# The up-projection of a feed-forward layer as seven block products per column pair, with the gated rows kept in memory

## Chip, core and metric

The kernel runs on one core of a Trainium2 chip. The metric is device microseconds of one execution. Engines are named as the profile names them: PE is the tensor engine (PEld its weight loads), DVE the vector engine, ACT the scalar engine, POOL the GpSimd engine, SP the engine that issues most transfers.

## What is computed

One layer of a decoder trunk for 1024 prompt tokens and 8 decode rows: a normalised input x, three token mixers, a layer norm, then a gated feed-forward with a causal convolution of width 3 over its up-projected rows, and a second layer norm. The change is in the feed-forward; the reference has it as

```
def conv_ffn(x, buf, w_up, conv_w, conv_b, w_down):
    hup = x @ w_up
    ext = jnp.concatenate([buf.astype(hup.dtype), hup], axis=1)
    c = ext[:, 0:L] * conv_w[0] + ext[:, 1:L + 1] * conv_w[1] + ext[:, 2:L + 2] * conv_w[2] + conv_b
    a, b = jnp.split(c, 2, axis=-1)
    return (jax.nn.gelu(a) * b) @ w_down, ext[:, -(CONV_WIDTH - 1):]
...
    x = layer_norm(ALPHA * x + f, ln2_g, ln2_b)
```

x has 1024 features, hup 2 x 2816 columns, so there are 22 feature tiles of 128 for a and 22 for b. All data is float32.

## The kernel before

Tokens stand side by side in 1032 columns (1024 and the 8 decode rows), features on the 128 partitions. Every float32 factor of a large product is split into two parts of 12 bits, hi and lo: ACT copies the source to the short type (hi), DVE or POOL subtracts it (lo). A product is then three matmuls, hi by hi, hi by lo, lo by hi. xhi and xlo hold x's parts in eight feature tiles.

The program is written as a list of units. A unit is 128 output columns: for each of three token chunks (384, 384, 264) it adds eight k-tiles times three matmuls into one PSUM bank, and then a function empties the bank. run_units goes through them; between matmuls it loads weights (a 512 KB piece, SP), splits them (whi on ACT, line 180; wlo, line 181, mostly on DVE, on POOL for a few stages) and advances side work, given as generators in lanes. The order on each engine is the order in which the program writes it; each engine works through its queue in order. Three banks, tag "d", go round under the units; units marked wide use others as well.

The stages: memory keys and values, input projection and mLSTM, attention, gates, pooling, w_o with the first layer norm, feed-forward, second layer norm. The gates are written to memory by POOL's transfers (line 1117) and come back later. to_features writes the normalised rows into xhi and xlo.

In the feed-forward an up unit (up_unit) empties its bank twice on ACT, as hup (line 1490) and as cv with the convolution's last tap and bias (line 1491). convolved then adds the other taps on DVE (line 1503, two instructions of about 1023 columns, and two of 8 for the decode rows), takes gelu on ACT for the a tile (line 1506), multiplies on POOL for the b tile (line 1509), copies hup's last columns on POOL (line 1500) and splits the gated tile into GH (lines 1523, 1524), which stay in SBUF. Up units and down units are mixed: after four feature tiles' gates, eight down units of four k-tiles (36 matmuls each) add to z2 (lines 1539 to 1544). The pool named rows, 21 tiles of 128x1032, holds the gates, z2 and cv.

## Time and profile before

| What | us |
|---|---|
| median of 3 runs (2214.75 to 2216.33) | 2214.9 |
| span of the profiled execution | 2210.3 |
| PE busy in it | 2169.0 |
| DVE busy | 1207.6 |
| ACT busy | 826.1 |
| POOL busy | 364.5 |

The span runs from the first to the last instruction of the profiled execution, whose mean granted clock is 0.994. Rows of the chain of waits and of the timeline give the start in us, the duration in us, and what ran; xN means N instructions in a row. Groups give count, busy us and mean ns of one, then the idle time ahead of them and what ended it. Rows by window give, after the length, the sum busy and then PE, PEld, DVE, ACT and POOL, with the count of instructions in brackets, the granted clock, the share of transfer engines and GB/s. The feed-forward runs from about 1405 to 2118 us.

### The profile page before, as it was taken

How to read it: one execution, taken by the hardware profiler on the slowest of the kernel's cores; microseconds unless marked ns; L12 is line 12 of the kernel's file. 1: busy time of each engine (PE TensorE's matmuls, PEld its weight loads, DVE VectorE, ACT ScalarE, POOL GpSimd, SP SyncE). 2: the span in 40 equal slices, each digit the busy share in tenths (PEclk: the TensorE clock that was granted, in tenths of full speed). 3: DMA queues.
4: the chain of work that ended last, by engine and by line, in shares of the span. 5: the costliest groups of instructions: out<-in, count | busy, mean ns of one | idle time of the engine just before them, and what ended most of it. 6: DMA issues, size and time to landing. Idle time of an engine off the chain costs nothing.

```text
span 2210.3 us, 36109 instructions
## 1 busy us (share of the span) xinstructions
PE 2169.0 (98%) x14337; PEld 2140.7 (97%) x14337; DVE 1207.6 (55%) x2776; ACT 826.1 (37%) x1635; POOL 364.5 (16%) x523
## 2 busy tenths in 40 slices
PE   8999999999999999999999999999999999999996
PEld 7899999999999999999999999999999999999996
DVE  6834738383767765635335556644544343443457
ACT  4524343434457543442213333444142341423421
POOL 6301010101110000211004734101010010101104
PEclk9999999999999999999999999999999999999998
DMA  9131232223367664649653223311111111111112
GB/s 264 55 106 53 58 72 53 63 61 70 90 187 260 193 193 159 217 173 339 189 165 103 87 77 86 87 49 49 42 45 49 49 49 48 39 52 45 49 49 77
DMA packets 267795, 229.50 MB, mean 104 GB/s; under 512 B 15669, under 2 KB 245863, under 8 KB 267611
## 3 DMA queue, kind: packets, MB, share of 16 engines
q1 hardware_dynamic: 261291, 208.12, 31.4%
q0 software_dynamic: 6336, 19.09, 2.3%
q8 instruction: 112, 1.84, 0.3%
q14 instruction: 56, 0.46, 0.1%
HBM read 177.13 MB, written 50.64 MB: 103 GB/s over the span
## 4 chain that ended last, share of the span: by engine, by line
PE 88%; DVE 4%; issue 3%; DMA 1%; SPq 1%; ACT 1%; POOL 1%; ACTq 0%; DVEq 0%; POOLq 0%
PE pd L250 79%; PE ps L668 1%; PE ps L669 1%; PE ps L670 1%; DMA Cs<-in_state_C_dram 1%; SPq L171 1%; DVE xlo L387 1%; PE ps L692 1%; PE ps L1086 1%; PE ps L878 1%; PE ps L382 0%; DVE st L358 0%; DVE xhi L386 0%; DVE wlo L181 0%; PE ps L688 0%
## 5 line engine op out<-in xcount | busy, mean ns | idle before, releaser
L250 PE MATMUL pd<-xhi,whi 128*128 128x384 f32 (+1 forms) x2784 | 897.3, 322 | 0.6 <-ACT gf L541 0.6
L250 PE MATMUL pd<-xlo,whi 128*128 128x384 f32 (+1 forms) x2784 | 895.0, 321 | 0.0
L250 PE MATMUL pd<-xhi,wlo 128*128 128x384 f32 (+1 forms) x2784 | 891.2, 320 | 0.0
L250 PEld LDWEIGHTS pd<-xhi,whi 128*128 128x128 f32 x2784 | 524.5, 188 | 1.9 <-ACT gf L541 0.8
L250 PEld LDWEIGHTS pd<-xlo,whi 128*128 128x128 f32 x2784 | 524.9, 189 | 0.1
L250 PEld LDWEIGHTS pd<-xhi,wlo 128*128 128x128 f32 x2784 | 524.3, 188 | 0.0
L181 DVE TENSOR_TENSOR wlo<-raw,whi 128x512 fp32r<-128x512 f32 (+1 forms) x326 | 227.0, 730 | 437.2 <-ACT whi L180 430.6
L180 ACT ACTIVATE whi<-raw 128x512 fp32r<-128x512 f32 (+1 forms) x382 | 219.4, 620 | 271.6 <-PE pd L250 201.4
L1490 ACT ACTIVATE hup<-pd 128x384 f32<-128x384 f32 (+1 forms) x132 | 60.4, 458 | 277.9 <-PE pd L250 277.7
L1503 DVE SCALAR_TENSOR_TENSOR cv<-hup,colB,cv 128x1023 f32<-128x1023 f32 x88 | 112.7, 1281 | 1.6
L1544 DVE TENSOR_TENSOR z<-pd,z 128x384 f32<-128x384 f32 (+3 forms) x120 | 59.5, 511 | 82.6 <-PE pd L250 82.6
L1500 POOL COPY tl<-hup 128x10 f32<-128x10 f32 x44 | 8.4, 192 | 519.6 <-ACT hup L1490 519.6
L366 POOL TENSOR_TENSOR rs<-rs,half 128x1 f32<-128x1 f32 (+2 forms) x60 | 38.0, 633 | 340.2 <-DVE rs L365 330.1
L1491 ACT ACTIVATE cv<-pd,colB 128x384 f32<-128x384 f32 (+1 forms) x132 | 83.6, 633 | 0.0
L181 POOL TENSOR_TENSOR wlo<-raw,whi 128x512 fp32r<-128x512 f32 x56 | 76.3, 1386 | 41.4 <-ACT whi L180 41.4
L1117 POOL DMA_DIRECT2D gD<-ch x60 | 32.8, 547 | 293.5 <-ACT ch L1116 274.4
L1509 POOL TENSOR_TENSOR cv<-cv,cv 128x1032 f32<-128x1032 f32 x22 | 53.1, 2414 | 112.6 <-DVE cv L1503 97.0
L250 PE MATMUL pd<-mh,whi 128*128 128x392 f32 (+2 forms) x192 | 62.7, 326 | 0.6 <-ACT mh L1338 0.6
L250 PE MATMUL pd<-ml,whi 128*128 128x392 f32 (+2 forms) x192 | 61.8, 322 | 0.1
L250 PE MATMUL pd<-mh,wlo 128*128 128x392 f32 (+2 forms) x192 | 61.5, 321 | 0.0
L1116 ACT ACTIVATE ch<-pd,colA 128x384 f32<-128x384 f32 (+1 forms) x60 | 32.7, 545 | 67.1 <-PE pd L250 56.2
L662 ACT ACTIVATE hh<-ps,colA 128x128 fp32r<-128x128 f32 x64 | 23.1, 360 | 79.7 <-DVE hh L663 75.0
(731 smaller groups left out, 4040.9 us busy)
## 6 DMA issues: line engine op xcount, KB each, us to landing
raw<-in_w_in_dram SPq DMA_DIRECT2D x72, 512.0 KB
raw<-in_w_up_dram SPq DMA_DIRECT2D x44, 512.0 KB
raw<-in_w_down_dram SPq DMA_DIRECT2D x22, 512.0 KB
raw<-in_w_o_dram SPq DMA_DIRECT2D x18, 512.0 KB
mx<-mixD SPq DMA_DIRECT2D x16, 516.0 KB
raw<-in_w_mem_kv_dram SPq DMA_DIRECT2D x16, 512.0 KB
Cs<-in_state_C_dram SPq DMA_DIRECT2D x32, 256.0 KB
out_dram<-Cs SPq DMA_DIRECT2D x32, 256.0 KB
```

Source lines behind the costliest of these rows:

```text
L180: nc.scalar.activation(s.hi[:, ks], s.raw[:, ks], AF.Copy)
L181: (nc.gpsimd if s.pool else nc.vector).tensor_sub(s.lo[:, ks], s.raw[:, ks], raw_f(s.hi[:, ks]))
L250: nc.tensor.matmul(p[:u.m, :n], lhsT=a, rhs=b, start=j == 0, stop=j == len(seq) - 1)
L366: nc.gpsimd.tensor_tensor(out=rs[:n], in0=rs[:n], in1=half[:n], op=OP.pow)
L662: nc.scalar.activation(hi, src, AF.Copy, scale=scale)
L1116: nc.scalar.activation(t[:, :n], p[:, :n], AF.Identity, bias=bias)
L1117: nc.gpsimd.dma_start(GD[b][f][:, c0:c0 + n], t[:, :n])
L1490: nc.scalar.activation(rw[:, c0:c0 + n], p[:, :n], AF.Copy)
L1491: nc.scalar.activation(cc[:, c0:c0 + n], p[:, :n], AF.Identity, bias=colB[:, 132 + ft:133 + ft], scale=colB[:, 88 + ft:89 + ft])
L1503: nc.vector.scalar_tensor_tensor(a, b[0], b[1], a, op0=OP.mult, op1=OP.add)
L1509: nc.gpsimd.tensor_mul(cc, CA.pop(j), cc)
L1544: nc.vector.tensor_add(Z2[f][:, cs], p[:, :n], Z2[f][:, cs])
```

## The change

The first three feature tiles' up units (NSTD) stay as they were. Each of the other 19 pairs, column tile a and column tile b of one feature tile j, is now one product of a 2 x 2 block form: the rows of w_up are halved (512 features each), the columns are the a and the b tile, the tokens are halved (516 columns). Seven block products take the place of eight, in the form with shared sums: sums of weight blocks are built per pair on POOL (lines 1604, 1605, 1607, 1610 of the changed kernel), sums of token blocks once, on DVE and POOL (g_parts), each then split into two parts. Each product is done for two quarters s of 258 columns: seven products of four k-tiles and three matmuls (line 1733). Products 2 and 3 add onto the banks of products 1 and 5. ACT and DVE then empty the banks with the partial results as second factor (lines 1740 to 1755), into two hup tiles. The convolution starts from hup alone (line 1499 in ACT, 1505 on DVE, 1509 gelu, 1512 product on POOL).

The token sums overwrite half of xhi and xlo (last_part) and x1D, a copy in memory of the normalised rows, is written by ACT's transfers during the first layer norm. The gated tiles go to memory (gD, SP). When all pairs are done, the down products run in six groups: a group's gates come back into a stage tile, are split into xhi and xlo, and z2 starts from x1D. The weights' pool is one tag of eight tiles; rows is closed when the four last standard units begin, and five smaller pools take its place. Transfers of rowsA, of the gates and of y1 are issued by ACT and no longer by POOL, that of mixD by SP.

```diff
...
+NSTD = 3
+SEQ = (1, 6, 7, 5, 2, 4, 3)
+HB, HT = 258, 516
...
-    wp = ctx.enter_context(tc.tile_pool(name="weights", bufs=2))
-    hp = ctx.enter_context(tc.tile_pool(name="rows", bufs=NH))
+    wp = ctx.enter_context(tc.tile_pool(name="weights", bufs=8, side="right"))
+    sp = ctx.enter_context(tc.tile_pool(name="small", bufs=4))
+    early = ExitStack()
+    hp = early.enter_context(tc.tile_pool(name="rows", bufs=NH))
     pp = ctx.enter_context(tc.tile_pool(name="psum", bufs=1, space=bass.MemoryType.PSUM))
...
-            nc.gpsimd.dma_start(rowsA[dst:dst + n], as_rows(src))
+            nc.scalar.dma_start(rowsA[dst:dst + n], as_rows(src))
...
+            if spill:
+                nc.scalar.dma_start(spill[f][:, c0:c0 + n], tmp[:, :n])
...
-                nc.gpsimd.dma_start(GD[b][f][:, c0:c0 + n], t[:, :n])
+                nc.scalar.dma_start(GD[b][f][:, c0:c0 + n], t[:, :n])
...
+    def g_conv(j, isb, rw):
+
+        ft = j + NFF * isb
+        if j % 2 == 0 and not isb:
+            TL[j // 2] = sp.tile([128, 4, 10], F32, tag="tl", bufs=2, name=nm("tl"))
+        tl = TL[j // 2]
+        cc = R("cv")
+        w0, w1 = colB[:, ft:ft + 1], colB[:, 44 + ft:45 + ft]
+        nc.scalar.activation(cc, rw, AF.Identity, bias=colB[:, 132 + ft:133 + ft], scale=colB[:, 88 + ft:89 + ft])
+        nc.gpsimd.tensor_copy(tl[:, 2 * isb + j % 2, :], rw[:, T - 2:])
+        yield
+        steps = ((cc[:, 1:T], (rw[:, :T - 1], w1)), (cc[:, 2:T], (rw[:, :T - 2], w0)),
+                 (cc[:, T:], (stT[:, ft, 1, :], w1)), (cc[:, T:], (stT[:, ft, 0, :], w0)))
+        for i, (a, b) in enumerate(steps):
+            nc.vector.scalar_tensor_tensor(a, b[0], b[1], a, op0=OP.mult, op1=OP.add)
+            if i in (0, 3):
+                yield
+        if not isb:
+            nc.scalar.activation(cc, cc, AF.Gelu_apprx_tanh)
+            CA[j] = cc
+            return
+        nc.gpsimd.tensor_mul(cc, CA.pop(j), cc)
+        if j % 2:
...
+        yield
+        yield
+        nc.sync.dma_start(gD[j], cc)
...
+    def split_weights(o, key, src, pool):
+        slot = slots.pop(0)
+        t = (wp if slot == "w" else place["ex"]).tile([128, 1024], F32R, tag="w", name=nm("whl"))
+        n = src.shape[1]
+        hi, lo = t[:, :n], t[:, 512:512 + n]
+        nc.scalar.activation(hi, src, AF.Copy)
+        (nc.gpsimd if pool else nc.vector).tensor_sub(lo, src, raw_f(hi))
+        o.w[key] = [x.rearrange("p (k c) -> p k c", c=128) for x in (hi, lo)] + [slot]
+
...
+    def prepare():
+
+        if made["obj"] == made["load"] or not slots:
+            return False
+        o = wq[made["obj"]]
+        key = o.steps[made["step"]]
+        if o.pair:
+            add, sub = nc.gpsimd.tensor_add, nc.gpsimd.tensor_sub
+            if made["step"] == 0:
+                o.s = [wf_tile(), wf_tile()]
+            a11, a21, a22, a12 = o.f
+            s1, s2 = o.s
+            if made["step"] == 0:
+                add(s1, a21, a22)
+                sub(s2, s1, a11)
+            elif made["step"] == 1:
+                sub(a21, a11, a21)
+            split_weights(o, key, {1: a11, 6: s2, 7: a21, 5: s1, 2: a12, 4: a22, 3: a12}[key], key in (2, 4))
+            if key == 4:
+                sub(a12, a12, s2)
+        else:
+            split_weights(o, key, o.f[key], False)
+        made["step"] += 1
+        if made["step"] == len(o.steps):
+            made["step"] = 0
+            made["obj"] += 1
+            made["live"] -= o.nf
+            load_weights()
+        return True
+
+    def ready_weights(o, key):
+        while key not in o.w:
...
+    def x_part(m, k, s):
+        if m in (6, 7, 4):
+            a, b = TX[m]
+            return a[:, k, s * HB:(s + 1) * HB], b[:, k, s * HB:(s + 1) * HB]
+        kk, c0 = {1: (0, 0), 2: (4, 0), 3: (4, HT), 5: (0, HT)}[m]
+        c0 += s * HB
+        return xhi[:, kk + k, c0:c0 + HB], xlo[:, kk + k, c0:c0 + HB]
...
+    def open_ffn():
         wait_for("ln11")
...
+        flush()
+        ph.close()
+        early.close()
+        for name in ("t", "wf", "ex", "rc", "st"):
+            place[name] = ph.enter_context(tc.tile_pool(name=f"ffn_{name}", reuse_waits="tile",
+                                                        bufs={"t": 3, "wf": NWF, "ex": 2, "rc": 5, "st": 2}[name]))
+        cur[0] = place["rc"]
+        slots[:] = ["x", "x"]
+        made["live"] = 6
+        load_weights()
+        side.add(0, "parts", g_parts())
+        side.add(1, "first", g_first())
...
+    on(units[n0 + 4], "before", open_ffn)
...
+    def g_parts():
...
+        for k in range(4):
+            (h11, l11), (h12, l12), (h21, l21), (h22, l22) = (
+                [raw_f(x[:, k + 4 * a, b * HT:(b + 1) * HT]) for x in (xhi, xlo)] for a in range(2) for b in range(2))
+            t1, t2, t3 = wf_tile(HT), wf_tile(HT), wf_tile(HT)
+            T1.append(t1)
+
+            def split(m, src):
+                nc.scalar.activation(TX[m][0][:, k], src, AF.Copy)
+                V.tensor_sub(TX[m][1][:, k], src, raw_f(TX[m][0][:, k]))
+
+            P.tensor_sub(t3, h22, h12)
+            P.tensor_add(t3, t3, l22)
+            P.tensor_sub(t3, t3, l12)
+            V.tensor_sub(t1, h12, h11)
+            V.tensor_add(t1, t1, l12)
+            yield 2.0
+            V.tensor_sub(t1, t1, l11)
+            V.tensor_sub(t2, h22, t1)
+            V.tensor_add(t2, t2, l22)
+            yield 2.2
+            split(6, t2)
+            yield 1.5
+            split(7, t3)
+            P.tensor_sub(t2, h21, t2)
+            P.tensor_add(t2, t2, l21)
+            yield 2.0
+            split(4, t2)
...
+    def last_part():
+        for k in range(4):
+            h, l = xhi[:, k, HT:], xlo[:, k, HT:]
+            nc.scalar.activation(h, T1[k], AF.Copy)
+            nc.vector.tensor_sub(l, T1[k], raw_f(h))
+        made["live"] -= 4
...
+    class Pair:
+        def __init__(self, j):
+            self.j, self.hooks = j, {}
+            a, b = j * 128, FF + j * 128
+            q = lambda k, c: w_up[0, k * 512:(k + 1) * 512, c:c + 128].rearrange("(k p) c -> p k c", p=128)
+            self.w = Weights([q(0, a), q(0, b), q(1, b), q(1, a)], True)
+            wq.append(self.w)
...
+    def run_pair(u):
+        out = None
+        for s in range(2):
+            c1, c2 = slice(s * HB, (s + 1) * HB), slice(HT + s * HB, HT + (s + 1) * HB)
+            bank = {}
+            for i, m in enumerate(SEQ):
+                ready_weights(u.w, m)
+                onto = {2: 1, 3: 5}.get(m)
+                p = bank[m] = bank[onto] if onto else (
+                    pp.tile([128, 512], F32, tag="d", bufs=3, name=nm("pd")) if m in (1, 5) else PS("pd"))
+                wh, wl = u.w.w[m][:2]
+                for k in range(4):
+                    xh, xl = x_part(m, k, s)
+                    for n, (a, b) in enumerate(((wh, xh), (wh, xl), (wl, xh))):
+                        nc.tensor.matmul(p[:, :HB], lhsT=a[:, k], rhs=b, start=onto is None and k + n == 0,
+                                         stop=k == 3 and n == 2, skip_group_check=onto is not None)
+                if s:
+                    release(u.w, m)
+                p = p[:, :HB]
+                if m == 1:
+                    t1 = small("t1")
+                    nc.scalar.activation(t1, p, AF.Copy)
+                elif m == 6:
+                    u2 = small("u2")
+                    nc.vector.tensor_add(u2, p, t1)
+                elif m == 7:
+                    u3 = small("u3")
+                    nc.vector.tensor_add(u3, p, u2)
+                else:
+                    if out is None:
+                        out = [R("hup"), R("hup")]
+                    if m == 2:
+                        nc.scalar.activation(out[0][:, c1], p, AF.Copy)
+                    elif m == 3:
+                        nc.vector.tensor_add(out[0][:, c2], p, u2)
+                    else:
+                        nc.vector.tensor_add(out[1][:, c1 if m == 4 else c2], p, u3)
+                if (s, i) in u.hooks:
+                    u.hooks[s, i]()
+                post[:] = [g for g in post if next(g, g) is not g]
+                prepare()
+                side.advance(12 * HB / 2180.0)
+
+        def both():
+            yield from g_conv(u.j, 0, out[0])
+            yield from g_conv(u.j, 1, out[1])
+        post.append(both())
+
+
...
+    def stage_load(gi, parts):
+        j0, nk = GROUPS[gi]
+        if gi not in stage:
+            stage[gi] = place["t"].tile([128, 4, TT], F32, tag="t", name=nm("stage"))
+        for c0, c1 in parts:
+            for k in range(nk):
+                nc.sync.dma_start(stage[gi][:, k, c0:c1], gD[j0 + k][:, c0:c1])
+
+    def stage_split(gi, k, c0, c1):
+        kk = (gi % 2) * 4 + k
+        nc.scalar.activation(xhi[:, kk, c0:c1], stage[gi][:, k, c0:c1], AF.Copy)
+        nc.vector.tensor_sub(xlo[:, kk, c0:c1], stage[gi][:, k, c0:c1], raw_f(xhi[:, kk, c0:c1]))
...
+    def begin_down():
+        load_z2([0])
+        stage_load(0, ((384, TT),))
+        load_z2(range(1, 8))
+        side.add(0, "stages", g_stages())
+
+    pairs[-1].hooks = {(1, 1): lambda: stage_load(0, ((0, 384),)),
+                       (1, 5): lambda: stage_split(0, 0, 0, 384),
+                       (1, 6): lambda: [stage_split(0, k, 0, 384) for k in range(1, 4)]}
+    downs[0].before = begin_down
...
+            z = Z2[u.f][:, c0:c0 + n]
+            if u.gi == 0:
+                nc.vector.scalar_tensor_tensor(z, z, ALPHA, p[:, :n], op0=OP.mult, op1=OP.add)
+            else:
+                nc.vector.tensor_add(z, p[:, :n], z)
...
     run_units(2)
+    made["open"] = True
+    side.finish("parts")
+    slots.extend("www")
+    last_part()
+    load_weights()
+    for u in pairs:
+        run_pair(u)
+    for u in downs:
+        run_down(u)
...
```

POOL in the middle of the pairs, before (two up units; tl is the tail copy, cv the convolution):

```order
398 L1500 COPY tl_18417<-hup_18415 128x10
399 L1500 COPY tl_18417<-hup_18528 128x10
400 L1500 COPY tl_18417<-hup_18994 128x10
401 L1509 TENSOR_TENSOR cv_2932_18995<-cv_2875_18416,cv_2932_18995 128x1032
402 L1500 COPY tl_18417<-hup_19090 128x10
```

and of the change, one pair:

```order
399 L1500 COPY tl_19738<-hup_19525 128x10
400 L1500 COPY tl_19738<-hup_19526 128x10
401 L1512 TENSOR_TENSOR cv_19793<-cv_19739,cv_19793 128x1032
402 L1588 TENSOR_TENSOR whl_19875<-wf_19404,whl_19875 128x512
403 L1588 TENSOR_TENSOR whl_19893<-wf_19402,whl_19893 128x512
404 L1610 TENSOR_TENSOR wf_19404<-wf_19404,wf_19683 128x512
405 L1604 TENSOR_TENSOR wf_19935<-wf_19663,wf_19665 128x512
406 L1605 TENSOR_TENSOR wf_19936<-wf_19935,wf_19661 128x512
407 L1607 TENSOR_TENSOR wf_19663<-wf_19661,wf_19663 128x512
```

Behind the gate's product POOL now has six instructions on weights in each pair, where it had none (wf is a weight block or a sum of such, whl the two split parts).

DVE in a pair of the change, from the last sum of one pair into hup (L1753) through both convolutions of its two tiles; before, the convolutions (L1503) had only weight splits and the gate's split beside them:

```order
2236 L1753 TENSOR_TENSOR hup_19009<-pd_19128,u_3075_19103 128x258
2237 L1588 TENSOR_TENSOR whl_19204<-wf_18884,whl_19204 128x512
2238 L1743 TENSOR_TENSOR u_3097_19239<-pd_19226,t_3093_19220 128x258
2239 L1505 SCALAR_TENSOR_TENSOR cv_19223<-hup_19009,colB,cv_19223 128x1023
2240 L1746 TENSOR_TENSOR u_3099_19255<-pd_19242,u_3097_19239 128x258
2241 L1505 SCALAR_TENSOR_TENSOR cv_19223<-hup_19009,colB,cv_19223 128x1022
2242 L1505 SCALAR_TENSOR_TENSOR cv_19223<-stT,colB,cv_19223 128x8 x2
2243 L1755 TENSOR_TENSOR hup_19274<-pd_19260,u_3099_19255 128x258
2244 L1505 SCALAR_TENSOR_TENSOR cv_19277<-hup_19010,colB,cv_19277 128x1023
2245 L1755 TENSOR_TENSOR hup_19274<-pd_19294,u_3099_19255 128x258
2246 L1505 SCALAR_TENSOR_TENSOR cv_19277<-hup_19010,colB,cv_19277 128x1022
```

The sums that empty the banks (L1743 to L1755) now stand between the convolution's steps.

SP between the last pair and the first down group, with what each transfer waits for:

```order
699 L1577 DMA wf_22060<-in_w_down_dram 128x4x128 [waits DMAHW6_49,DVE_49]
700 L1801 DMA z_3478_22062<-x1D_129_230 128x1032 [waits DMAHW7_49,PE_49]
701 L1789 DMA stage_21949<-gD_145_239 128x648 [waits DMAHW0_49]
702 L1789 DMA stage_21949<-gD_147_240 128x648 [waits DMAHW1_49]
703 L1789 DMA stage_21949<-gD_149_241 128x648 [waits DMAHW2_49]
704 L1789 DMA stage_21949<-gD_151_242 128x648 [waits DMAHW3_49]
```

The gates' second and third chunk (648 columns) come behind a weight load that waits for DVE; before, this place had no transfer of gates.

271 lines of the change are left out of this document (154 added, 117 removed).

## The prediction

> **What bounds the kernel now.** I read the busy shares first, then the chain of waits over the feed-forward stage (1470 to 2130 us), then busy time by window, then single instructions in order of time.
>
> ```profile
> PE 2169.0 (98%) x14337; PEld 2140.7 (97%) x14337; DVE 1207.6 (55%) x2776; ACT 826.1 (37%) x1635; POOL 364.5 (16%) x523
> by line: PE pd L250 96.5%; issue 5.7%; PE ps L1513 0.7%; DVE cv L1503 0.4%; POOL cv L1509 0.4%; DVE wlo L181 0.1%; ACT whi L180 0.1%; ACT cv L1491 0.1%; ACT hup L1490 0.1%; POOLq L1509 0.0%
> ...
> 1481.19 45.27 PE pd L250 x288
> ...
> 1526.91 90.59 PE pd L250 x576
> ...
> 1526.90:1617.50 90.60, 90.60 (x579) 90.49 (x578) 48.83 (x83) 24.27 (x44) 5.59 (x6) 1.00 0.16 47
> ```
>
> The chain is TensorE's from end to end. 288 matmuls are four up units of 72, so a unit takes 45.27/4 = 11.32 us and its two columns (a and b of one feature tile) 22.64. The last row gives, after the span, the busy time of PE, PEld, DVE, ACT, POOL: POOL works 5.6 of 90.6 us here, so it hardly meets DVE. That is what the change alters.
>
> **TensorE's part.** The changed pair has 2 token halves x 7 products x 12 = 168 matmuls of 258 columns; two units had 144, two thirds of 384 columns. How far apart matmuls start:
>
> ```profile
> 14.96 0.28 PE L250 MATMUL pd<-memT0h,whi 128*128 128x256 f32 x1
> ...
> 17.45 0.28 PE L250 MATMUL pd<-memT0h,whi 128*128 128x256 f32 x1
> ...
> 1704.61 0.28 PE L250 MATMUL pd<-g4h,whi 128*128 128x264 f32 x1
> ...
> 1706.07 0.34 PE L250 MATMUL pd<-g4h,whi 128*128 128x384 f32 x1
> ...
> 1708.18 0.34 PE L250 MATMUL pd<-g4h,whi 128*128 128x384 f32 x1
> ```
>
> 21 of 256 columns take 2.49 us (0.1186 each), 12 of 264 take 1.46 (0.1217), 12 of 384 take 2.11 (0.176). 258 columns lie between the first two; I take 0.1195, near 256. A pair is 168 x 0.1195 = 20.1 us of TensorE (19.9 to 20.4). 19 pairs: 19 x (20.1 - 22.64) = **-48 us** if TensorE never waits.
>
> **What else a pair needs.** Row durations of the same or the nearest forms (columns: busy us, mean ns, idle before):
>
> ```profile
> L181 DVE TENSOR_TENSOR wlo<-raw,whi 128x512 fp32r<-128x512 f32 x116 | 74.9, 687 | 188.9 <-ACT whi L180 187.9
> L1544 DVE TENSOR_TENSOR z<-pd,z 128x264 f32<-128x264 f32 x24 | 10.3, 431 | 19.1 <-PE pd L250 19.1
> L1506 ACT ACTIVATE cv<-cv 128x1032 f32<-128x1032 f32 x21 | 22.4, 1068 | 22.2 <-DVE cv L1503 22.2
> L1509 POOL TENSOR_TENSOR cv<-cv,cv 128x1032 f32<-128x1032 f32 x21 | 50.7, 2414 | 108.0 <-DVE cv L1503 92.4 <-issue 10.4 <-ACT cv L1491 5.2
> ```
>
> ```profile
> 1600.42 2.59 DVE L1503 SCALAR_TENSOR_TENSOR cv<-hup,colB,cv 128x1023 f32<-128x1023 f32 x2
> 1602.93 0.48 DVE L1503 SCALAR_TENSOR_TENSOR cv<-stT,colB,cv 128x8 f32<-128x8 f32 x2
> ...
> 1610.53 1.29 DVE L181 TENSOR_TENSOR wlo<-raw,whi 128x512 fp32r<-128x512 f32 x2 [1.04 <-ACT whi L180]
> 1611.74 2.60 DVE L1503 SCALAR_TENSOR_TENSOR cv<-hup,colB,cv 128x1023 f32<-128x1023 f32 x2
> ```
>
> Back to back, a convolution costs DVE 2.51 + 0.48 = 2.99 us and a low-part subtraction 1.21/2 = 0.61. Per pair DVE has 5 low parts (3.0), 10 sums out of PSUM at 0.42 (4.2) and two convolutions (6.0): 13.2 us. POOL has 4 weight sums and 2 low parts, the gate's product (2.41) and two tails of 0.19. Its 128x512 price and what it does to DVE stand in the stretch around 1400 us, the one place where both are busy:
>
> ```profile
> 1395.91 2.54 POOL L181 TENSOR_TENSOR wlo<-raw,whi 128x512 fp32r<-128x512 f32 x2 [1.57 <-ACT whi L180]
> ...
> 1399.29 2.53 POOL L181 TENSOR_TENSOR wlo<-raw,whi 128x512 fp32r<-128x512 f32 x2 [0.29 <-ACT whi L180]
> 1406.42 2.64 POOL L181 TENSOR_TENSOR wlo<-raw,whi 128x512 fp32r<-128x512 f32 x2 [4.60 <-ACT whi L180]
> ```
>
> ```profile
> 1400.33 0.42 DVE L1386 SCALAR_TENSOR_TENSOR ztmp<-xhi,pd 128x256 f32<-128x256 f32 x1 [1.13 <-PE pd L250]
> 1400.78 1.39 DVE L1390 SCALAR_TENSOR_TENSOR z<-xlo,ztmp 128x128 f32<-128x128 f32 x2
> ...
> 1405.54 0.49 DVE L1390 SCALAR_TENSOR_TENSOR z<-xlo,ztmp 128x128 f32<-128x128 f32 x2
> ...
> 1407.96 1.53 DVE L387 TENSOR_TENSOR xlo<-tmp,xhi 128x384 fp32r<-128x384 f32 x1
> 1409.41 0.35 DVE L386 CAST xhi<-tmp 128x384 fp32r<-128x384 f32 x1
> 1409.79 0.56 DVE L387 TENSOR_TENSOR xlo<-tmp,xhi 128x384 fp32r<-128x384 f32 x1
> ```
>
> POOL's 128x512 takes 1.27 us, so 6 x 1.27 + 2.41 + 0.38 = 10.4 us a pair. DVE's L390-type pair, whose inputs all lie in SBUF, takes 0.49 us at 1405.54 and 1.39 at 1400.78: it ends 0.35 after POOL's second subtraction does (1399.29 + 2.53 = 1401.82). L387 takes 0.56 alone and 1.53 at 1407.96, again ending 0.43 after POOL (1406.42 + 2.64 = 1409.06). L1386 in the same stretch, with one input from PSUM, keeps its 0.42. So a DVE instruction with two SBUF inputs doesn't run beside a POOL instruction, it waits for its end; PSUM sums go on.
>
> The Trainium skill, page "SBUF — State Buffer", section "Who interferes with whom", gives the same as a rule: a DVE instruction with two SBUF inputs contends with a GpSimd instruction that reads SBUF, one with at most one doesn't, and the loser is blocked for the whole instruction. These rows agree. By that rule all of a pair's POOL work excludes DVE's convolutions and low parts, and it speaks against putting weight sums on POOL beside them; without the rule and the rows the pair would be the first rival below.
>
> **The loop of a steady pair.** The two engines' excluded work is 10.4 + 3.0 + 6.0 = 19.4 us of 20.1, if no gap were left. But both run in order and POOL's product is queued ahead of its six weight instructions. From one pair's last sum into hup (product 3, second half) to the next pair's: ACT's bias pass 1.07; first convolution with one PSUM sum queued inside it, 2.99 + 0.42 (two more hide under ACT's passes); gelu and the second bias pass on ACT, 2.14, DVE idle but for such a sum; second convolution with one sum, 3.41; POOL's product 2.41; then six POOL instructions, 7.6, alternating with four of DVE's low parts, 2.4, each behind the other; the last sum 0.42. That is **22.9 us**, and DVE's low part of product 3 stands in its queue ahead of the sums, which wait with it. A hand-over costs about 0.1 us (the convolution ends at 1603.41; POOL's product starts at 1603.58); a few are on the loop: 23.2. TensorE then stands in front of product 3 in each pair, whose bank DVE must first read (the sum of product 5). 19 x (23.2 - 22.64) = **+11** in place of -48. Bounds: 20.1 (all hidden) and 26.4, every DVE and POOL instruction in turn (13.2 + 10.4) with 2.8 of ACT between; I stay near the loop, since its rows are of the same forms.
>
> **The opening.** Once, four standard units (4 x 11.32 = 45.3 us) cover the building of the token sums: 20 POOL instructions of 128x516, 36 of DVE with two SBUF inputs. Their first waits for a buffer that gate 0's transfer to memory frees. In the last gate of the profile the work from the evacuation to the product's end takes 7.6 us (first and last row), here some 2 more with the gelu's table and the queue; the transfer 4 to 6.5:
>
> ```profile
> 2111.00 0.39 ACT hup L1490
> ...
> 2116.19 2.41 POOL cv L1509
> ```
>
> ```profile
> gD<-ch POOLq DMA_DIRECT2D x40, 192.0 KB, 4.0
> ...
> mixD<-y1r POOLq DMA_DIRECT2D x8, 516.0 KB, 6.5
> ```
>
> So it begins about 14 us into the four units. Behind it: DVE 36 x 0.61 + 9 weight parts 5.5 + 3 convolutions 9.0 = 36.5; POOL 20 x 1.27 + 6 x 1.27 + 2.41 = 35.4, of which some 3 can come later. One after the other: 14 + 69 = 83 us, while TensorE reaches the first pair's product 5, which needs the last of them, at 45.3 + 4.3 = 49.6. **+34 us.** Below: side by side the 36.5 would end at 51, but ACT's evacuations stand behind the splits and three banks run out: 10 to 24. Above: 45 with the hand-overs.
>
> **From pairs to the down groups.** Before, gates stayed in SBUF. Now the first group's second and third chunk come from memory: SP's loads stand behind a weight load that waits for DVE's last low part, which waits for the end of the last pair. About 4 us after that end the loads start, behind a 516 KB z tile and 256 KB of weights; by the 6.5 us of the 516 KB row and two splits (ACT 1.07, DVE 0.7 scaled) the chunk is ready some 14 us after the end; TensorE has 2.1 us of products (12 x 0.176) and a short wait before. **+10** (5 to 15). Later groups are loaded a group (45 us) ahead: +1.
>
> **Start and spills.** The column loads go from POOL to ACT, eight of them ahead of the memory's evacuation, and the last waits until the first x tile has landed:
>
> ```profile
> 6.34 1.21 ACT L446 ACTIVATE memT0h<-ps 128x256 fp32r<-128x256 f32 x4 [4.04 <-PE ps L444]
> ...
> 15.20 1.28 DVE L358 BATCH_NORM_STATS2 st<-x 128x6 f32<-128x512 f32 x2
> ```
>
> ```profile
> PE ps L382 <- DVE x L370: 6.7, 2, 4.3
> ```
>
> ACT's first evacuation moves from 6.3 to about 15; up to 4.3 us of it falls into a wait that TensorE has anyway. **+4** (0 to 9). Gate spills and the layer norm's spill on ACT hold that engine behind SP's transfers, with three banks of cover: **+3** (0 to 10); what hides them is TensorE's queue of finished banks, and without it each costs its transfer's wait.
>
> **Sum**, against the profile's own 2210.3 us (4.6 under the median): 11 + 34 + 10 + 1 + 4 + 3 = +63, a span of 2273, a time of **2278 us**.
>
> **Rivals.** *Nothing excludes* (chance 0.20): POOL and DVE run side by side, and the loop closes after the product (12.5) with 7.6 of POOL, the last split and sum: 20.4 us a pair. Then 19 x (20.4 - 22.64) = -43, the opening 24, the rest 18: -1, **2214 us**; with an opening of 10 it is 2200. For it: POOL lets DVE in between two instructions (the cast before 1407.96). Against it: the five stretched rows. It decides once a pair's loop is under 20.1. *Full turn-taking* (0.12): low parts on both engines hold up the PSUM sums, 26.4 a pair: 19 x 3.8 = +71, opening 40, rest 18: +129, **2344**; it needs the PSUM sums never to overlap POOL, against L1386's 0.42.
>
> **Chances and range.** The forecast has 0.68, its own range 2240 to 2315 (pairs 22 to 25, opening 20 to 45). The first rival's lower half lies outside the whole range, as does most of the second: **2212 to 2322**. A difference below 0.2% (4.4 us) can't be told from none. Faster: half the first rival and a little of the forecast, 0.11; same 0.07; slower 0.82.
>
> **What would show it.** Right: pair periods near 23 us in the chain with TensorE waiting for DVE's sum of product 5; DVE low parts of 1.2 us and more beside POOL's sums; a gap of some 30 us before the first pair's product 5; about 10 before the second chunk of the first down group. Wrong: pairs at 20 us with low parts of 0.6, or TensorE waiting on weights or transfers inside the pairs.

## The result, and the profile after

The changed kernel takes **2268.2 us** (2266.5 to 2268.5), the kernel before, on the same chip, 2215.3: a ratio of 1.0237, with a 95% interval of 1.0222 to 1.0251, so 53 us slower. The profiled execution spans 2264.8 us, 54.5 over the 2210.3 of before, with a mean granted clock of 0.979 (before 0.994). Forecast were 2278 us and a span of 2273.

Of the page, the busy times and the shares of the chain of waits:

```profile
PE 2150.9 (95%) x14793; PEld 2110.8 (93%) x14793; DVE 1391.3 (61%) x3005; ACT 835.1 (37%) x1590; POOL 519.5 (23%) x557
...
PE 57%; issue 18%; POOL 9%; DVE 8%; DMA 4%; ACT 3%; SPq 0%; ACTq 0%; POOLq 0%; DVEq 0%
```

TensorE is busy for 18 us less than before and the span is 54 longer. POOL works 155 us more, DVE 184. Of the chain over the whole span TensorE has 57%; POOL and DVE together have 17%, and the 18% of "issue" is time in which an engine waited for nothing that the profile shows.

The waits of TensorE, with the total, how often, and the longest:

```profile
PE pd L1733 <- DVE hup L1755: 23.1, 14, 1.7
PE pd L258 <- ACT hup L1534: 17.4, 3, 10.5
PE pd L1833 <- ACT xhi L1793: 8.4, 2, 7.6
PE ps L451 <- DVE memT0l L454: 8.3, 1, 8.3
PE pd L1733 <- ACT xhi L1695: 7.0, 1, 7.0
PE ps L387 <- DVE x L375: 5.9, 2, 4.0
...
PE pd L1733 <- DVE xlo L1696: 3.8, 3, 2.5
```

The first row is the pairs; the second, the fifth and the last are the opening; the third is the passage to the down groups; the fourth and the sixth are the start. By window (length, then sum and count for PE, PEld, DVE, ACT, POOL, granted clock, transfer share, GB/s), for the opening, steady pairs and the passage:

```profile
1480.00:1550.00 70.00, 41.94 (x240) 40.36 (x239) 55.85 (x55) 24.23 (x43) 46.55 (x32) 0.81 0.19 54
1600.00:1700.00 100.00, 94.96 (x754) 92.95 (x754) 75.19 (x106) 40.13 (x63) 50.91 (x38) 0.97 0.22 65
1980.00:2000.00 20.00, 16.62 (x91) 15.41 (x92) 13.91 (x22) 9.27 (x11) 0.49 (x1) 0.81 0.94 368
```

TensorE is busy for 41.9 of the 70 us of the opening, and its clock is 0.81 there. In the steady pairs it is busy for 95%.

From instructions that both traces have (the first evacuations of v and of hup, the last evacuation of the standard units, the first down product), the 54.5 us divide like this:

| Stretch | predicted | measured |
|---|---|---|
| start, to the first v (121.4 to 128.4) | +4 | +7.0 |
| from there to the first hup (1300.8 to 1307.4) | +3 | +6.6 |
| opening, first hup to the last of the standard units (73.6 to 109.3) | +34 | +35.7 |
| 19 pairs (430.2, as 19 x 22.64, to 425.9) | +11 | -4.3 |
| passage and down groups (what is left) | +11 | +9.5 |

The 22.64 of a pair before leaves out the transposes of hup's last columns, which come in every second pair: by the rows of the chain shown above, four units of 45.27 us begin 45.72 apart (1481.19 to 1526.91). Nine such times lie in the stretch, about 4 us. Counted with them, the 19 pairs took 434 us before and came to -8, and what is left to +13.5.

### The profile page after: what moved, and what is told of

It reads as the page before. It is cut to its first block, busy times and chain, and to the rows that moved or that the text cites. A ratio compares the mean times of both kernels' runs of the same rounds, so it can differ in the third digit from the quotient of the medians.

```text
span 2264.8 us, 37937 instructions
## 1 busy us (share of the span) xinstructions
PE 2150.9 (95%) x14793; PEld 2110.8 (93%) x14793; DVE 1391.3 (61%) x3005; ACT 835.1 (37%) x1590; POOL 519.5 (23%) x557
## 3 DMA queue, kind: packets, MB, share of 16 engines
q1 hardware_dynamic: 283307, 239.83, 35.4%
## 4 chain that ended last, share of the span: by engine, by line
PE 57%; issue 18%; POOL 9%; DVE 8%; DMA 4%; ACT 3%; SPq 0%; ACTq 0%; POOLq 0%; DVEq 0%
PE pd L258 47%; POOL cv L1512 2%; PE ps L675 1%; PE ps L676 1%; PE ps L677 1%; PE pd L1733 1%; POOL wf L1607 1%; DMA gD<-cv 1%; POOL wf L1605 1%; POOL wf L1610 1%; POOL wf L1604 1%; DVE xlo L394 1%; DVE wlo L189 1%; DMA stage<-gD 1%; POOL whl L1588 1%
## 5 line engine op out<-in xcount | busy, mean ns | idle before, releaser
L258 PE MATMUL pd<-xhi,whi 128*128 128x384 f32 (+1 forms) x1872 | 607.2, 324 | 17.9 <-ACT hup L1534 17.4
L258 PE MATMUL pd<-xlo,whi 128*128 128x384 f32 (+1 forms) x1872 | 605.0, 323 | 0.0
L258 PE MATMUL pd<-xhi,wlo 128*128 128x384 f32 (+1 forms) x1872 | 602.0, 322 | 0.0
L1733 PE MATMUL pd<-xhi,whl 128*128 128x258 f32 x1216 | 243.1, 290 | 32.0 <-DVE hup L1755 23.1
L1833 PE MATMUL pd<-xhi,whl 128*128 128x384 f32 (+3 forms) x1056 | 251.2, 323 | 13.8 <-ACT xhi L1793 8.4
L1733 PEld LDWEIGHTS pd<-xhi,whl 128*128 128x128 f32 x1216 | 198.7, 193 | 38.0 <-DVE hup L1755 26.6
L1833 PEld LDWEIGHTS pd<-xhi,whl 128*128 128x128 f32 x1056 | 184.9, 190 | 16.3 <-ACT xhi L1793 9.3
L1733 PE MATMUL pd<-xlo,whl 128*128 128x258 f32 x608 | 174.7, 287 | 3.8 <-DVE xlo L1696 3.8
L1733 PE MATMUL pd<-tx,whl 128*128 128x258 f32 x1368 | 177.0, 283 | 0.0
L1833 PE MATMUL pd<-xlo,whl 128*128 128x384 f32 (+3 forms) x528 | 170.6, 323 | 0.7 <-DVE xlo L1794 0.5
L1733 PEld LDWEIGHTS pd<-tx,whl 128*128 128x128 f32 x1368 | 170.2, 190 | 0.0
```

Of the source, the lines that this page charges most:

```text
L258: nc.tensor.matmul(p[:u.m, :n], lhsT=a, rhs=b, start=j == 0, stop=j == len(seq) - 1)
L1733: nc.tensor.matmul(p[:, :HB], lhsT=a[:, k], rhs=b, start=onto is None and k + n == 0, stop=k == 3 and n == 2, skip_group_check=onto is not ...
L1833: nc.tensor.matmul(p[:, :n], lhsT=a[:, k], rhs=b, start=k + i == 0, stop=k == nk - 1 and i == 2)
```

## Experiments

Times are medians, ratios against the kernel before on the same chip. Three lengths are read from each trace. The opening is counted from the first evacuation of hup (L1534) to the first of a pair's product 1 (L1740), the pair from one gate's product to the next over whole numbers of pairs (another choice of pairs moves the mean by up to 0.03), the down products from the start of the first to that of the last.

| Version | time | ratio, interval | opening | pair | down products |
|---|---|---|---|---|---|
| changed kernel | 2268.2 | 1.0237 (1.0222, 1.0251) | 111.3 | 22.44 | 279.6 |
| no weight sums | 2225.9 | 1.0050 (1.0035, 1.0065) | 102.7 | 20.37 | 281.5 |
| weight sums on DVE | 2250.9 | 1.0162 (1.0147, 1.0177) | 109.5 | 21.47 | 280.3 |
| gates loaded earlier | 2271.5 | 1.0252 (1.0235, 1.0269) | 111.3 | | 279.7 |
| row loads by POOL | 2264.2 | 1.0218 (1.0202, 1.0233) | 111.3 | | 278.7 |
| all pair work on DVE | 2230.2 | 1.0069 (1.0054, 1.0084) | 106.0 | 20.33 | 278.7 |
| token sums on DVE | 2269.3 | 1.0249 (1.0232, 1.0266) | 106.9 | 22.43 | 282.3 |
| gates and two z tiles earlier | 2272.4 | 1.0258 (1.0243, 1.0274) | 109.9 | | 282.7 |
| combination | 2215.7 | 1.0002 (0.9993, 1.0011) | 99.9 | 20.37 | 280.2 |
| combination, four standard pairs | 2198.5 | 0.9926 (0.9911, 0.9940) | 106.0, with 22.6 of the fourth | | 279.6 |
| z tiles one by one | 2266.5 | 1.0228 (1.0211, 1.0245) | 111.4 | | 276.0 |
| last version | 2191.2 | 0.9889 (0.9875, 0.9904) | 105.9, with 22.6 of the fourth | 20.35 | 272.9 |
| last version, copies by POOL | 2200.7 | 0.9931 (0.9914, 0.9947) | 104.2, with 22.6 of the fourth | | 278.0 |

The theory at the start: in the pairs, the two engines' turn-taking sets the period and TensorE waits for it; the opening is DVE's and POOL's work beyond its cover; the passage is the order of SP's transfers; the start is the row loads' place on ACT. The rivals were that TensorE itself needs the 22 us, and that transfers set the passage whatever their order.

### The pairs: without the weight sums

```diff
-                add(s1, a21, a22)
-                sub(s2, s1, a11)
-                sub(a21, a11, a21)
-                sub(a12, a12, s2)
-            split_weights(o, key, {1: a11, 6: s2, 7: a21, 5: s1, 2: a12, 4: a22, 3: a12}[key], key in (2, 4))
+            split_weights(o, key, {1: a11, 6: a22, 7: a21, 5: a21, 2: a12, 4: a22, 3: a12}[key], key in (2, 4))
```

This version leaves the four sums of weight blocks out; products 6, 7, 5 and 3 use unsummed blocks, with the same matmuls and splits.

> The four weight sums of each pair on POOL are left out (products 6, 7, 5 and 3 take a raw block instead, so hup is not the reference's); everything else stays. Theory (a loop of DVE and POOL, which exclude each other, sets the pair at 22.4 us): 4 x 1.27 = 5.1 us leave the loop, which falls to about 17.4, so TensorE's 20.1 us decides; 19 x 2.3 = -44, and 2 to 5 us less in the opening: about 2220 us. Rival 1 (the pair is long because of TensorE itself or of its transfers, and POOL is beside the path): no change, 2268 +- 4. Rival 2 (only the opening suffers from POOL): -5, 2263.

Measured 2225.9, 42 us less. The row of the window 1580 to 1900:

```profile
1580.00:1900.00 320.00, 320.00 (x2676) 319.42 (x2676) 244.62 (x371) 141.19 (x221) 91.12 (x80) 1.00 0.28 82
```

TensorE is busy for all 320 us at clock 1.00, while DVE and POOL have 245 and 91. The pair falls from 22.44 to 20.37. In the traces the stretch from the first pair's product 1 to the first down product falls from 423.9 to 390.4, 33.5 us (some 16 steady pairs of 2.07; the first and the last pair differ little), and the opening by 8.6. Together that is 42.1, as much as the medians differ; the traced execution was longer elsewhere (from v to hup 1312.0 us, in the changed kernel 1307.4), so that its span fell by 35.4. So TensorE does not need the 22 us. This run also takes away the sums that ACT's splits wait for, and so can't tell the engine from the work; the run with everything on DVE, below, keeps the work. The period takes two values in turn, 20.1 and 20.65, since every second pair has four more matmuls, the transposes of the tails (L1516); the expectation for everything on DVE, below, took the larger for the mean.

### The pairs: weight sums on DVE

```diff
-            add, sub = nc.gpsimd.tensor_add, nc.gpsimd.tensor_sub
+            add, sub = nc.vector.tensor_add, nc.vector.tensor_sub
```

> The four weight sums of a pair on DVE instead of POOL; the result is the same. Theory (exclusion): POOL loses 4 x 1.27 us, DVE gains 4 x 0.61; both lie on the same loop, so it shortens by 2.6 to about 19.8 and TensorE's 20.1 decides: 19 x 2.2 = -42, opening -3, about 2223 us. Rival (no exclusion; DVE, at 16.8 of 22.4 us the busier engine, is what is full): DVE gets longer by 2.4 us a pair, 0 to +46: 2268 to 2314.

Measured 2250.9: faster, as no rival had it, but by 17 us instead of 45. The pair takes 21.47. Two rows of this kernel's order of time point to why:

```profile
1692.40 3.01 POOL L1588 TENSOR_TENSOR whl<-wf,whl 128x512 fp32r<-128x512 f32 x2
...
1694.19 1.77 DVE L1610 TENSOR_TENSOR wf<-wf,wf 128x512 f32<-128x512 f32 x1 [0.32 <-POOL whl L1588]
```

POOL still has two low parts, queued behind the gate's product. DVE's sum L1610 waits for the first of them and then takes 1.77 us beside the second, where such a sum takes 0.68 once POOL is done (L1604 at 1697.33); what DVE has behind it waits too. Sums that are free of POOL are not enough as long as one link of the loop lies on it.

### The pairs: everything on DVE

```diff
-        nc.gpsimd.tensor_mul(cc, CA.pop(j), cc)
+        nc.vector.tensor_mul(cc, CA.pop(j), cc)
...
-            add, sub = nc.gpsimd.tensor_add, nc.gpsimd.tensor_sub
+            add, sub = nc.vector.tensor_add, nc.vector.tensor_sub
...
-            split_weights(o, key, {1: a11, 6: s2, 7: a21, 5: s1, 2: a12, 4: a22, 3: a12}[key], key in (2, 4))
+            split_weights(o, key, {1: a11, 6: s2, 7: a21, 5: s1, 2: a12, 4: a22, 3: a12}[key], False)
```

> The pairs' four weight sums, the two low parts of products 2 and 4 and the gate's product all on DVE; POOL keeps only two tail copies a pair. Theory (what costs is that POOL and DVE exclude each other, so DVE alone is faster than both): DVE has 13.2 + 4 x 0.61 + 2 x 0.61 + 1.2 = 18.0 us a pair, under TensorE's 20.65 (the period that the run without sums showed), nothing waits for POOL; period 20.65, 19 x (22.44 - 20.65) = 34 less than the changed kernel's 2268: 2234, and a few less for the first pair: 2230. Rival (the in-order queue of DVE, now at 87%, is itself the loop, as the half gain of the run with only the sums on DVE would suggest): period 21.4 or more, 2248 to 2255.

Measured 2230.2, as the theory had it. The window 1580 to 1900 of this kernel:

```profile
1580.00:1900.00 320.00, 320.00 (x2677) 319.36 (x2676) 273.18 (x484) 139.84 (x221) 11.41 (x32) 1.00 0.29 82
```

and the low parts of the window 1640 to 1703, with mean ns:

```profile
L1588 DVE TENSOR_TENSOR whl<-wf,whl 128x512 fp32r<-128x512 f32 x21 | 14.3, 682 | 1.3 <-ACT whl L1587 1.3
```

DVE does the whole of the work of two engines in 273 of 320 us, and TensorE never waits. In the changed kernel the same low part took 1502 ns on the mean. DVE alone is faster than DVE and POOL together: the rival, that DVE's own queue is the loop, falls.

### The opening: token sums on DVE

```diff
-        V, P = nc.vector, nc.gpsimd
+        V = P = nc.vector
```

> Only the opening: the 20 token-sum instructions of POOL go to DVE as well; the pairs stay as changed. Theory (in the opening each of the two engines' instructions stretches to about 1.65 us because they take turns, so the two are no faster than DVE alone at 0.7): DVE has 56 x 0.7 = 39, its weight parts 5 and three convolutions 9, from 1479 to 1533 where the last token part now ends at 1540: 7 to 12 less, 2258. Rival 1 (the gap is set by ACT's evacuation queued behind splits that wait for a chain of sums, whichever engine makes them): within 3 of 2268. Rival 2 (two engines side by side do gain, DVE alone is longer): 2272 to 2280.

Measured 2269.3, which can't be told from the changed kernel. In the trace the opening is 4.4 us shorter (106.9), but the stretch from v to hup came out 3.2 longer in this execution and the down products 2.7. TensorE's three waits for a bank in the opening come to 16.7 us (17.4 in the changed kernel), those at the first pair to 10.2 (10.8):

```profile
PE pd L258 <- ACT hup L1534: 16.7, 3, 10.6
```

ACT's first wait for a sum is 16.9 us in both. So rival 1 describes it better than the theory: with one kind of work taken off POOL alone TensorE waits almost as long as before.

### Start: row loads issued by POOL again

```diff
-            nc.scalar.dma_start(rowsA[dst:dst + n], as_rows(src))
+            nc.gpsimd.dma_start(rowsA[dst:dst + n], as_rows(src))
```

> The eight rowsA loads at the start go back from ACT to POOL, as before the change. Theory (they hold ACT's first evacuation until the eighth may start): the 8.3 us wait at the first transposes goes, and the stages up to 600 us start 7 us earlier: about 2261 us. Rival (the start is later because of where the loads' bytes or the other engines stand): 2268, no change.

Measured 2264.2. The evacuations of v in this kernel, with their first and last start (128.4 and 484.3 in the changed kernel):

```profile
L650 DVE TENSOR_SCALAR v<-pd,colA x24: 481/607/619, 121.7 to 477.6; 128x384 f32<-128x384 f32 x16, 128x264 f32<-128x264 f32 x8
```

The first v comes at 121.7 again (before the change 121.4): all 7 us of the start are the loads' place on ACT. In the median 4 of them show.

### The passage: three orders of the same transfers

First, the gates' second and third chunk loaded with the first:

```diff
-    pairs[-1].hooks = {(1, 1): lambda: stage_load(0, ((0, 384),)),
+    pairs[-1].hooks = {(1, 1): lambda: stage_load(0, ((0, 384), (384, TT))),
...
-        stage_load(0, ((384, TT),))
```

> The second and third chunk of the first down group's gates are loaded together with the first chunk, inside the last pair, instead of after it. Theory (the passage costs 10.6 us because these loads are issued 5.6 us after the last pair's end and land 5.6 later): TensorE's gap of 7.6 us and the slow matmuls behind it go, -8 to -10: about 2259 us. Rival (the gap is bandwidth: weights, z and gates together): the same bytes only come earlier and the gap stays, or half of it: 2264 to 2268.

Measured 2271.5: no gain. Rows in order of time, of SP, DVE and TensorE:

```profile
1982.97 4.43 SPq L1801 DMA_DIRECT2D z<-x1D  x8
1988.42 0.56 DVE L1841 SCALAR_TENSOR_TENSOR z<-z,pd 128x384 f32<-128x384 f32 x1 [8.21 <-DMA z<-x1D]
...
1989.78 0.69 PE L1833 MATMUL pd<-xlo,whl 128*128 128x384 f32 x1 [8.18 <-DVE xlo L1794]
```

The gates came in time, but the first z tile was now loaded behind six weight pieces. DVE stood 8.2 us for it, with the low parts of the next chunk queued behind. Then the z tiles were moved too:

```diff
-    pairs[-1].hooks = {(1, 1): lambda: stage_load(0, ((0, 384),)),
+    pairs[-1].hooks = {(1, 1): lambda: stage_load(0, ((0, 384), (384, TT))),
+                       (1, 2): lambda: load_z2([0, 1]),
...
-        load_z2([0])
-        stage_load(0, ((384, TT),))
-        load_z2(range(1, 8))
+        load_z2(range(2, 8))
```

> The passage from pairs to down groups: the gates' second and third chunk are loaded with the first, inside the last pair, and the first two z tiles right behind them, ahead of the weight loads. In the run with the earlier chunks alone DVE stood 8.2 us for the z tile that then came behind six weight loads, with the low parts of the next chunk in its queue. Theory (the whole gap is the order of SP's loads): 7 to 9 less than 2268: 2260. Rival (another load, or the splits themselves, ACT 0.73 and DVE 0.78 for each of eight 128x648 pieces, takes the place): 2265 to 2270.

Measured 2272.4: no gain again. Two windows:

```profile
1970.00:1980.00 10.00, 7.72 (x38) 5.16 (x37) 7.72 (x14) 7.04 (x12) 0.33 (x2) 1.00 0.98 308
1990.00:2000.00 10.00, 8.46 (x54) 7.98 (x52) 3.94 (x6) 4.27 (x5) 0.00 (x0) 1.00 1.02 407
```

At both ends of the passage the transfer engines are busy, with 308 and 407 GB/s, and the wait is only cut into pieces (DVE waits 3.5 us for a z tile, TensorE 3.5 for low parts, and slow matmuls follow). So not the order alone. Last, with the gates as in these two runs, one z tile ahead of the weight loads and the others one by one, each a unit ahead of its use:

```diff
+    for f in range(1, 7):
+        downs[f].before = lambda f=f: load_z2([f + 1])
...
-        load_z2([0])
-        stage_load(0, ((384, TT),))
-        load_z2(range(1, 8))
+        load_z2([1])
+        Z2["t", 1] = place["t"].tile([128, 4, TT], F32, tag="t", name=nm("z2"))
```

> The changed kernel with the passage of the run with earlier gates and z tiles, but only the first z tile ahead of the weight loads, and the other seven one by one, each a down unit ahead of its use. Theory (the passage is bound by bytes: the transfer engines are 0.86 to 1.05 busy from 1970 to 2000, with gates, eight z tiles, weights and the next group's gates all issued in 20 us, so the order didn't matter): the first z tile and the gates land some 5 us earlier, 2268 - 6 = 2262, and the transfer share of 1980 to 2000 falls under 0.7. Rival (ACT's and DVE's splits of the gates, and the wait for weights on SP, hold it): 2268 to 2273.

Measured 2266.5, 1.7 under the changed kernel, which the intervals don't tell apart; under the run with two z tiles earlier (2272.4), from which it differs only in the z tiles, it is 5.9, and those intervals just touch. The window 1980 to 1990:

```profile
1980.00:1990.00 10.00, 5.11 (x18) 3.95 (x19) 4.50 (x7) 3.10 (x4) 0.00 (x0) 0.75 1.10 361
```

The transfer share, 1.10 here and 0.87 in the next 10 us, didn't fall under 0.7; the down products took 276.0 us, where the changed kernel has 279.6 and the run with two z tiles earlier 282.7. Gates of two groups, one z tile and weights are still due at once. That bytes set the passage fits all three runs, but it isn't shown: no run left the bytes out.

### The combination

The edits of "all pair work on DVE", "token sums on DVE" and "gates and two z tiles earlier", with the row loads, the gate spills and the y1 spills issued by POOL as before the change:

```diff
-                nc.scalar.dma_start(GD[b][f][:, c0:c0 + n], t[:, :n])
+                nc.gpsimd.dma_start(GD[b][f][:, c0:c0 + n], t[:, :n])
...
-            nc.scalar.dma_start(y1D[f][:, c0:c0 + n], t[:, :n])
+            nc.gpsimd.dma_start(y1D[f][:, c0:c0 + n], t[:, :n])
```

> The three edits of this job together, with the row loads and the gate and y1 spills issued by POOL again as before the change. If the parts add: 2268 - 38 (pairs) - 10 (opening) - 8 (passage) - 4 (row loads) - 4 (spills) = 2204, faster than the kernel before (2215). Rival (the gains overlap: DVE, which then carries all sums, is the bound of the opening, and the row and spill edits give half): 2220 to 2230, still slower than before.

Measured 2215.7, between the two, and the same as the kernel before (0.9993 to 1.0011). By the traces the pairs gave 33.6 us, the start 7.5, and the opening 11.4, where the two edits alone had given 5.3 and 4.4. The passage gave nothing, and the spills gave nothing that shows: from v to hup it is 1309.2 here, 1307.4 in the changed kernel, 1300.8 before. (In the other traces it lies between 1307.3 and 1312.0, on whichever engine the spills are, but for the last one below.) What is left against the pairs' gain is the opening, in which DVE works 57.8 of 70 us and TensorE 56.1:

```profile
1480.00:1550.00 70.00, 56.10 (x329) 54.72 (x328) 57.79 (x91) 26.32 (x46) 3.42 (x4) 0.85 0.20 61
```

So a fourth pair was left as standard units, to cover it:

```diff
-NSTD = 3
+NSTD = 4
...
-            yield 2.0
+            yield 3.00
```

(and so for the other steps of the token sums, each 1.5 times as far apart).

> The combination of the last job, and a fourth pair of units left as before, with the token sums paced one and a half times slower: six standard units cover the opening where four did. In that combination 97.9 us lie between the first and the last evacuation of the standard units' hup, 73.3 before the change. Theory (DVE's own work in the opening, some 60 us, is more than four units of 11.3 cover; six give 68): 24.6 of stall falls to about 5, the fourth pair costs 22.64 - 20.35 = 2.3 more: 2216 - 20 + 2 = 2198, faster than the kernel before. Rival (the stall comes from ACT's evacuations standing behind splits that wait for a chain of sums, whatever the pace): 2214 to 2219.

Measured 2198.5, as expected. The same window:

```profile
1480.00:1550.00 70.00, 67.29 (x445) 66.84 (x444) 62.94 (x97) 31.72 (x54) 3.01 (x5) 0.96 0.21 62
```

TensorE is busy for 67.3 of 70 us. The opening without the fourth pair's 22.6 us is 83.4, against 99.9; so the rival, by which nothing changes whatever the pace, falls. But cover and pace were changed together. ACT's waits for the sums ahead of its splits (L1669 behind L1680) fall from 30.7 us to 6.9, so its evacuations hardly stand behind splits any more; whether the cover or the pace did it isn't shown. With the z tiles one by one as well:

> Both of this job's edits on top of the combination. If they add, 2198 - 6 = 2192, ratio to the kernel before 0.990. Rival (passage unchanged): 2198, ratio 0.992; if neither holds, 2216, ratio 1.000.

Measured 2191.2, 1.1% under the kernel before. Here the down products begin at 1903. The window from 1920 to 1930, first without the edit:

```profile
1920.00:1930.00 10.00, 7.38 (x48) 6.91 (x47) 4.08 (x5) 3.23 (x4) 0.00 (x0) 0.97 0.95 371
```

and with it:

```profile
1920.00:1930.00 10.00, 10.00 (x67) 9.85 (x67) 8.90 (x13) 5.04 (x7) 0.00 (x0) 1.00 0.54 192
```

The transfer share falls from 0.95 to 0.54, and TensorE is busy for 10.0 us instead of 7.4. Here the edit is worth 7 us, and the intervals don't overlap (0.9911 against 0.9904). The run that it is compared with has the two z tiles earlier; against the run with these alone it had given 5.9, and the down products fall by 6.7 us in both comparisons.

At last the transfers that were still not on POOL:

```diff
-                nc.scalar.dma_start(spill[f][:, c0:c0 + n], tmp[:, :n])
+                nc.gpsimd.dma_start(spill[f][:, c0:c0 + n], tmp[:, :n])
...
-                nc.sync.dma_start(mixD[0][f], Y1.pop(f))
+                nc.gpsimd.dma_start(mixD[0][f], Y1.pop(f))
...
-            nc.scalar.dma_start(x1D[f][:, T:], tmp[:, f])
+            nc.gpsimd.dma_start(x1D[f][:, T:], tmp[:, f])
```

> The last version, with the remaining transfers that the change moved off POOL or added ahead of the feed-forward issued by POOL as well: mixD (on SP since the change) and the copies of the normalised rows (on ACT). Even with the row loads and spills back on POOL, the stretch ahead of the feed-forward stays some 6 us longer than before the change (first evacuation of a gate to first evacuation of u: 588.4 against 584.4; first to last sum with x in w_o: 104.0 against 101.5). Theory (mixD holds SP ahead of weight loads, and the row copies hold ACT): these stretches come back by 4 or more, 2191 - 5 = 2186. Rival (something else, such as the one tag of eight weight tiles, makes them longer): 2189 to 2194, both stretches unchanged.

Measured 2200.7, slower: both missed. From the first gate to the first u it stays as it was (588.1), so mixD's queue is not what makes it longer; w_o's stretch grew from 104.0 to 110.0. There ACT waits for the copies (4.7 us, in the version before 0.6):

```profile
ACT tmp L389 <- DMA x1D<-tmp: 4.7, 3, 2.8
```

The copies of the normalised rows are better on ACT. (The down products took 5 us longer in this execution too.) What makes the stretch from v to hup 6 us longer than before the change stays open.

## Why the prediction was right, and which of its terms were not

**TensorE's part** held: 20.1 us were worked out from the spacing of 256- and 264-column matmuls, and the versions without waits take about 20.35. The 0.25 between are the transposes of the tails, 0.5 us in every second pair, which had been left out, as they had been out of the 22.64 before.

**The loop of a steady pair** held in every link but one. The changed kernel's trace over one period, all engines but TensorE, from one gate's product to the steps that lead to the next:

```profile
1607.03 2.42 POOL L1512 TENSOR_TENSOR cv<-cv,cv 128x1032 f32<-128x1032 f32 x1 [9.49 <-ACT whl L1587]
1607.15 2.85 DVE L1588 TENSOR_TENSOR whl<-wf,whl 128x512 fp32r<-128x512 f32 x1
...
1609.41 2.99 POOL L1588 TENSOR_TENSOR whl<-wf,whl 128x512 fp32r<-128x512 f32 x2
...
1612.36 1.28 POOL L1610 TENSOR_TENSOR wf<-wf,wf 128x512 f32<-128x512 f32 x1
...
1616.56 1.74 POOL L1607 TENSOR_TENSOR wf<-wf,wf 128x512 f32<-128x512 f32 x1
...
1617.41 1.44 DVE L1588 TENSOR_TENSOR whl<-wf,whl 128x512 fp32r<-128x512 f32 x1
...
1618.77 0.41 DVE L1753 TENSOR_TENSOR hup<-pd,u 128x258 f32<-128x258 f32 x1
...
1619.27 1.25 ACT L1499 ACTIVATE cv<-hup,colB 128x1032 f32<-128x1032 f32 x1
...
1620.56 1.28 DVE L1505 SCALAR_TENSOR_TENSOR cv<-hup,colB,cv 128x1023 f32<-128x1023 f32 x1 [0.44 <-ACT cv L1499]
...
1623.69 0.42 DVE L1755 TENSOR_TENSOR hup<-pd,u 128x258 f32<-128x258 f32 x1
```

POOL's product (2.42 us) and its six weight instructions run without a gap to 1618.30. DVE's low parts beside them take 1.4 to 2.9 us where they took 0.61. The last sum into hup (L1753) stands behind such a low part, and only then come ACT's pass, the first convolution, gelu, and so on to the next product:

```profile
1629.45 2.42 POOL L1512 TENSOR_TENSOR cv<-cv,cv 128x1032 f32<-128x1032 f32 x1 [9.49 <-issue]
```

That is 22.42 us after the first. TensorE pays in front of product 3 in most pairs, for the sum of product 5, which stands behind the convolution:

```profile
1624.16 0.39 PE L1733 MATMUL pd<-xhi,whl 128*128 128x258 f32 x1 [1.73 <-DVE hup L1755]
```

The step that was mis-sized is "six POOL instructions, 7.6, alternating with four of DVE's low parts, 2.4, each behind the other", 10.0 us. From the product's end (1609.45) to L1753's start (1618.77) it is 9.3 us, hand-overs among them. The rest of the loop, from that start to the next product, takes 10.7, where 0.42 + 1.07 + 3.41 + 2.14 + 3.41 = 10.45 and some hand-overs had been forecast. Where the two engines take turns they overlap a little, so the loop took 22.44 and not 23.2; the pairs came to -4.3 where +11 was forecast. This is the largest error, 15 us, where the whole forecast was off by 10.

The Trainium skill, page "SBUF — State Buffer", section "SBUF: two separate sides", says that the loser of such a meeting is blocked for the whole instruction. The trace agrees that one waits for the other, and shows a lower price than that: in the opening two such instructions meet over and over, DVE's of 0.70 us where it isn't held up (at 1479.03) and POOL's of 1.28 (as at 1612.36 above). Strict turns would give 1.98 for the two. DVE's come 1.69 apart, in three steps from 1479.76 to 1484.82:

```profile
1479.03 0.70 DVE L1675 TENSOR_TENSOR wf<-xhi 128x516 f32<-128x516 f32 x1 [5.49 <-DMA gD<-cv]
1479.76 1.67 DVE L1676 TENSOR_TENSOR wf<-wf,xlo 128x516 f32<-128x516 f32 x1
...
1484.82 1.64 DVE L1679 TENSOR_TENSOR wf<-xhi,wf 128x516 f32<-128x516 f32 x1
```

POOL's beside them take as long:

```profile
1480.95 1.61 POOL L1673 TENSOR_TENSOR wf<-wf,xlo 128x516 f32<-128x516 f32 x1
```

**Nothing excludes** and **full turn-taking**, the rivals, fell. The first had 20.4 us a pair with the work on both engines; there the pair took 22.44, with stretched low parts, and 20.33 with the same work on DVE alone. Against the second, PSUM sums on DVE kept 0.42 us.

**The opening** held in size (+35.7 against +34) and in its start: the first token sum begins at 1479.03, 14 us into the four units (which begin at about 1464.8, with the last evacuation of the unit ahead of them), once the gate has reached memory. Its place was wrong. The step said that TensorE would stop at the first pair's product 5; only 10.8 us of waits (L1695, L1696) are there. 17.4 lie earlier: ACT's evacuation stands behind a split that waits 16.9 us for the sums, and the banks run out, which the prediction had named only for its lower bound. The first 7.7 of these 16.9 us pass before the first sum can begin at 1479.03, while the first gate is finished and goes to memory. Most of the rest is slow matmuls behind these waits (last section). In order of time:

```profile
1488.22 0.63 ACT L1669 ACTIVATE tx<-wf 128x516 fp32r<-128x516 f32 x1 [16.91 <-DVE wf L1680]
...
1490.33 0.47 ACT L1534 ACTIVATE hup<-pd 128x384 f32<-128x384 f32 x1
...
1490.85 0.69 PE L258 MATMUL pd<-xhi,whi 128*128 128x384 f32 x1 [10.54 <-ACT hup L1534]
```

**The passage** held roughly in size (predicted 10 + 1, measured 9.5, or 13.5 with the transposes counted): the second chunk came 7.64 us late. TensorE's row in front of that chunk:

```profile
1983.03 0.69 PE L1833 MATMUL pd<-xhi,whl 128*128 128x384 f32 x1 [7.64 <-ACT xhi L1793]
```

The step gave the queue on SP as its cause; three other orders of the queue did not take the wait away, so that was not the whole cause; the rest of it stays open.

**The start** was under-sized: 4.3 us were to fall into a wait that TensorE has anyway, but that wait only shrank from 6.7 to 5.9, and nearly all of 7.0 counted.

**Spills** were under-sized (3 against 6.6), and their cause isn't borne out: with the gate and y1 spills back on POOL the stretch is as long (1307.3 to 1309.2 in three traces), and with the rows' copies there too it is longer. What makes it longer stays open.

The sum was right to 10 us of 53: the forecast's errors in the pairs (15 too high) and in the start and spills (7 too low) partly cancelled.

## What to carry to other kernels

Ahead of handing an engine's work to a neighbour, look in the trace for a stretch where both are busy: here DVE alone did all the work of a pair in 20.33 us, with time to spare (busy for 273 of 320 us), where DVE and POOL together took 22.44, since each stretched the other. A saving on the busiest engine is only worth what the in-order loop of its helpers leaves of it; follow one period round through every queue. Work that is done once needs cover of its own: a whole pair left in the old form, 2.3 us dearer by the estimate above, and a slower pace of the sums together took 16.5 us of the opening away.
